# Attention scores from rounded parts: three one-pass products, with the two halves of the array's rows in turns

## The chip, the cores and the metric

The kernel runs on one core of a Trainium2 chip. Its time is the device time of one execution in microseconds (us). Beside the timed runs there is one execution taken by the hardware profiler: its page and its trace are what is read here. TensorE is the matrix engine (PE for its matmuls, PEld for its loads of stationary operands), VectorE is DVE, ScalarE is ACT, GpSimd is POOL, SyncE is SP.

## The reference, cut to what matters

The program is a block with a mixer, a cross attention and 32 experts, and then a second block of four layers, on 256 tokens of 1024 features in fp32. The four layers are a differential attention, a latent attention, a dilated attention and a differential attention again, each followed by a feed-forward network. The change is in the differential and the dilated ones.

```
def diff_attention(...):                       # 16 query and key heads of 64, 8 value heads of 128
    s = einsum('bhqd,bhkd->bhqk', q, k)        # contraction over 64
    p = softmax(s).reshape(B, 8, 2, S, S)
    a = p[:, :, 0] - lam * p[:, :, 1]
    o = einsum('bhqk,bhkd->bhqd', a, v)

def dilated_attention(...):                    # 3 groups of 16 heads of 64
    for window, dilation in ((128, 1), (512, 4), (2048, 16)):
        s = einsum(..., q, k)                  # banded, within a phase of the dilation
        lse = logsumexp(s);  p = exp(s - lse);  o = p v
    o = sum over groups of softmax(lse over groups) * o
```

## The kernel before, in words

All projections are fp32 products taken as three products of rounded parts. `split` (L186 to L199) makes of fp32 weights a high part on ScalarE (`whi`, L197) and the rest on VectorE (`wlo`, L198), both in the type float32r, which TensorE takes in one pass; `mm3` (L201 to L206) adds high by high, high by low and low by high. What is multiplied by weights is split likewise when it leaves PSUM, by `evac_split` (L208): a copy on ScalarE (L211), a subtraction on VectorE (L212). The scores, though, are products of plain fp32 tiles: TensorE takes such a product as two instructions.

The contraction of a score is over 64 features, so that a head fills half of the rows of the array, and two heads lie in one tile of 128 partitions: rows 0 to 63 and rows 64 to 127.

A differential layer (`attn_a`) has a written plan of steps: F is a piece of a projection (12 matmuls with 512 columns), S the scores of a pair of heads and their softmax (L1018 issues the products), T the transposes of the probabilities, V the values, O their transposes, W a piece of the output projection. Queries and keys are projected by token, turned by `rope` and transposed on TensorE into PSUM (`transposed_heads`, L961), from where ScalarE copies them into `qT` and `kT` (L962). For each half of the tokens the products go to the two halves of the rows by turns.

The dilated layer (`attn_c`) works in four rounds of four heads. `proj` makes queries, keys and values of the round; `heads` is called after it for the round before. In `heads`, for each of two pairs of heads, for each head s and each half of the tokens t (a score block), the products of the three groups go into one bank of PSUM (L1282: 256 columns for the first group, 128 for the others); VectorE adds the mask and takes the maximum (L1286), negates it (L937), ScalarE takes the exponential (L939), VectorE divides by the sum (L1291, L1292), TensorE transposes (L1295) into `tpp`, and ScalarE copies the result out (L1296). When four blocks are done the values follow (L1304, `po`). I call one call of `heads` a heads pass. The score banks share a pool of two with other products, and the probability rows `pr` one of two buffers.

The order on each engine is not that of the code: a scheduler lays the instructions out when the program is built, by its own idea of when each can start, and each engine then works through its list strictly in order. So a change of one product's form moves the instructions around it.

Of the kernel before, what the change touches and what calls it, by code (L numbers as in the profile page):

```python
# [9 lines left out]
F32 = mybir.dt.float32  # L10
F32R = mybir.dt.float32r
# [25 lines left out]
class Norm:  # L37
    """rows += scale * acc, by halves of the columns; rows * g transposed into hh, hl (or the halves hh); the rstd per token."""
# [48 lines left out]
class LastNorm(Norm):  # L87
    """rows += scale * acc; rms(rows) * g to the output."""
# [25 lines left out]
class Kernel:  # L114
# [39 lines left out]
    def load(self, *names, cuts=1, inner=RAW, ordered=False):  # L154
        """Start the loads of units of weights, as they lie in DRAM, by turns in so many cuts (of each `inner` columns)."""
# [18 lines left out]
    def raw(self, name):  # L174
        """The next unit of weights."""
        if self.ahead:
            n, t = self.ahead.pop(0)
            assert n == tuple(name), (n, name)
            return t
        return self.load(name)[0]  # L180
# [5 lines left out]
    def split(self, view, shape):  # L186
        """fp32 weights as the exact sum of two float32r parts."""
# [13 lines left out]
    def mm3(self, out, lh, ll, rh, rl, start, stop):  # L201
        """out += (lh + ll)^T (rh + rl), the product of the two low parts aside."""
# [14 lines left out]
    def gain(self, ap, n=D, pool=None, tag="gain"):  # L217
        """A gain vector on every partition."""
# [4 lines left out]
    def rstd(self, ss, n, eps, w=1):  # L223
        """(ss / n + eps) ** -0.5 for [P, w]."""
# [7 lines left out]
    def squares(self, x, out):  # L232
        """out [128, 1] = the sum of the squares of x [128, 512]."""
# [7 lines left out]
    def spread(self, r):  # L241
        """[128, 2] by token -> [128, 256]: token along the row, on every partition."""
# [16 lines left out]
    def phase1(self):  # L259
        nc, tc, A = self.nc, self.tc, self.A  # L260
        with ExitStack() as ctx:
            # what is done with first lies lowest: there the experts' weights land
# [3 lines left out]
            # memory: its rows in a buffer of weights, keys feature-major  # L266
# [16 lines left out]
            # x, wholly normalised  # L283
# [23 lines left out]
    def blocks(self, unit, acc, hh, hl, k0, nk, ncol, first, last):  # L307
        """acc[t][n] += h[:, k-tiles] @ unit, unit [P, nk, ncol], activations stationary:
        the pieces of it by bank, each to be called."""
# [24 lines left out]
    def finish(self, banks, acc, norm):  # L334
        """The last products of a sum, a bank after the other, into the norm that follows."""
# [14 lines left out]
    def proj_B(self, unit, hh, hl, evac):  # L350
        """unit [P, 8, 512] as stationary: evac(bank, f0) gets [128 features, 2, 256 tokens]."""
# [15 lines left out]
    def mixer(self, ctx, hh, hl):  # L367
# [7 lines left out]
        vec = m.tile([P, 5, 4], F32, name="mixvec")   # conv taps, g_conv_out, g_fft_out by feature  # L375
# [3 lines left out]
        # u, token-major  # L379
# [1138 lines left out]
```

## Time and profile before

| | |
|---|---|
| median of 3 timed runs | 2599.82 us (2599.73 to 2604.89) |
| span of the profiled execution, first to last instruction | 2597.9 us |
| what lies around the span (median less span) | 1.9 us |
| TensorE busy | 2518.0 us, 97% |
| VectorE, ScalarE busy | 1119.9 us (43%), 954.6 us (37%) |
| DMA, share of 16 engines on the large queue | 65.3% |
| mean granted clock of TensorE | 0.997 |

The profiled execution is one of its own; its own time is known as its span. The busy shares are means over stages that differ: the experts (from 220 to 1180 us) move weights at over 420 GB/s, the second block moves 110 to 200 GB/s and works on TensorE. In a timeline each row has its start, its duration, engine, line, operation and tiles, and the number of like instructions that were merged; matmuls overlap, so the pitch from start to start tells what one costs, and a row's duration includes the tail of its last one.

### The profile page before, as it was taken

How to read it: one execution, taken by the hardware profiler on the slowest of the kernel's cores; microseconds unless marked ns; L12 is line 12 of the kernel's file. 1: busy time of each engine (PE TensorE's matmuls, PEld its weight loads, DVE VectorE, ACT ScalarE, POOL GpSimd, SP SyncE). 2: the span in 40 equal slices, each digit the busy share in tenths (PEclk: the TensorE clock that was granted, in tenths of full speed). 3: DMA queues.
4: the chain of work that ended last, by engine and by line, in shares of the span. 5: the costliest groups of instructions: out<-in, count | busy, mean ns of one | idle time of the engine just before them, and what ended most of it. 6: DMA issues, size and time to landing. Idle time of an engine off the chain costs nothing.

```text
span 2597.9 us, 34064 instructions
## 1 busy us (share of the span) xinstructions
PE 2518.0 (97%) x14280; PEld 1769.4 (68%) x14280; DVE 1119.9 (43%) x1716; ACT 954.6 (37%) x1583; POOL 123.8 (5%) x256
## 2 busy tenths in 40 slices
PE   8999999999999999999999999999999999999998
PEld 7885333333333333337799978998888899977997
DVE  5643211111111111126655656555555565566555
ACT  5451000000000001016644575445555544466443
POOL 0000000000000000002100020001111100021000
PEclk9999999999999999999999999999999999999999
DMA  9458999999999999994344433555334355543453
GB/s 359 143 190 322 379 427 417 424 428 428 427 428 427 427 428 427 370 421 173 115 180 176 182 129 134 195 195 195 127 134 146 134 199 183 199 164 113 174 192 114
DMA packets 55277, 677.03 MB, mean 261 GB/s; under 512 B 8112, under 2 KB 10800, under 8 KB 14416
## 3 DMA queue, kind: packets, MB, share of 16 engines
q1 hardware_dynamic: 54976, 674.29, 65.3%
q8 instruction: 114, 1.87, 0.3%
q10 hardware_dynamic: 144, 0.52, 0.1%
q14 instruction: 43, 0.35, 0.0%
HBM read 673.74 MB, written 1.05 MB: 260 GB/s over the span
## 4 chain that ended last, share of the span: by engine, by line
PE 47%; issue 8%; DVE 2%; ACT 1%; POOL 1%; DMA 1%; POOLq 0%; SPq 0%; ACTq 0%
PE pj L204 5%; PE pj L206 5%; PE pj L205 5%; PE pb L206 4%; PE pb L205 4%; PE pb L204 4%; PE acc L204 3%; PE acc L205 3%; PE acc L206 3%; PE sc L1282 1%; PE pg L672 1%; PE pu L672 1%; PE py L750 1%; DVE wlo L198 1%; PE po L1304 1%
## 5 line engine op out<-in xcount | busy, mean ns | idle before, releaser
L198 DVE TENSOR_TENSOR wlo<-raw,whi 128x1024 fp32r<-128x1024 f32 (+1 forms) x491 | 603.1, 1230 | 473.6 <-ACT whi L197 473.0
L197 ACT ACTIVATE whi<-raw 128x1024 fp32r<-128x1024 f32 (+1 forms) x491 | 515.1, 1050 | 602.1 <-PE pb L205 250.7
L204 PE MATMUL pb<-hhi,whi 128*128 128x256 f32 x1504 | 427.0, 284 | 0.5 <-ACT whi L197 0.4
L205 PE MATMUL pb<-hlo,whi 128*128 128x256 f32 x1504 | 426.5, 284 | 0.6 <-DVE hlo L212 0.6
L206 PE MATMUL pb<-hhi,wlo 128*128 128x256 f32 x1504 | 426.3, 283 | 0.0
L204 PEld LDWEIGHTS pb<-hhi,whi 128*128 128x128 f32 x1504 | 289.1, 192 | 3.2 <-ACT whi L197 0.8
L205 PEld LDWEIGHTS pb<-hlo,whi 128*128 128x128 f32 x1504 | 289.2, 192 | 2.6 <-DVE hlo L212 1.0
L206 PEld LDWEIGHTS pb<-hhi,wlo 128*128 128x128 f32 x1504 | 289.2, 192 | 0.6 <-DVE wlo L198 0.6
L672 PE MATMUL pg<-raw,xt 128*64 128x512 f32 x1024 | 240.4, 595 | 0.0
L750 PE MATMUL py<-raw,at 128*64 128x512 f32 x1024 | 240.3, 593 | 0.0
L672 PE MATMUL pu<-raw,xt 128*64 128x512 f32 x1024 | 232.2, 592 | 0.0
L204 PE MATMUL pj<-whi,hhi 128*128 128x512 f32 (+3 forms) x544 | 208.8, 384 | 0.4 <-ACT hhi L211 0.4
L206 PE MATMUL pj<-whi,hlo 128*128 128x512 f32 (+3 forms) x544 | 204.5, 376 | 0.0
L205 PE MATMUL pj<-wlo,hhi 128*128 128x512 f32 (+3 forms) x544 | 203.9, 375 | 0.0
L750 PEld LDWEIGHTS py<-raw,at 128*64 128x64 f32 x1024 | 85.2, 137 | 140.1 <-issue 140.1
L672 PEld LDWEIGHTS pu<-raw,xt 128*64 128x64 f32 x1024 | 76.7, 137 | 145.0 <-issue 144.9
L672 PEld LDWEIGHTS pg<-raw,xt 128*64 128x64 f32 x1024 | 76.1, 137 | 145.5 <-issue 144.8
L761 DVE TENSOR_TENSOR x<-pc,x 128x512 f32<-128x512 f32 x64 | 44.2, 692 | 257.6 <-PE pc L759 257.6
L204 PE MATMUL acc<-whi,ah 128*128 128x512 f32 x352 | 137.7, 391 | 0.0
L205 PE MATMUL acc<-wlo,ah 128*128 128x512 f32 x352 | 137.5, 391 | 0.0
L206 PE MATMUL acc<-whi,al 128*128 128x512 f32 x352 | 137.1, 389 | 0.0
L229 POOL TENSOR_TENSOR rr<-rv,mhalf 128x2 f32<-128x2 f32 (+1 forms) x36 | 26.3, 730 | 2203.9 <-DVE rv L227 2186.2
(297 smaller groups left out, 3164.2 us busy)
## 6 DMA issues: line engine op xcount, KB each, us to landing
raw<-in_w_moe SPq DMA_DIRECT2D x190, 2048.0 KB, 16.6
raw<-in_f_gu SPq DMA_DIRECT2D x44, 2048.0 KB, 8.4
raw<-in_f_out SPq DMA_DIRECT2D x24, 2048.0 KB, 8.2
raw<-in_a_qkv SPq DMA_DIRECT2D x12, 2048.0 KB, 8.3
raw<-in_c_qk SPq DMA_DIRECT2D x12, 2048.0 KB, 8.4
raw<-in_w_in SPq DMA_DIRECT2D x4, 2048.0 KB, 15.6
raw<-in_a_wo SPq DMA_DIRECT2D x4, 2048.0 KB, 7.9
raw<-in_c_v SPq DMA_DIRECT2D x4, 2048.0 KB, 8.4
```

Of the source, the lines that this page charges most:

```text
L197: nc.scalar.activation(h3, view, AF.Copy)
L198: nc.vector.tensor_tensor(l3, view, f32(h3), op=OP.subtract)
L204: mm(out, lh, rh, start=start, stop=False)
L205: mm(out, lh, rl, start=False, stop=False)
L206: mm(out, ll, rh, start=False, stop=stop)
L229: nc.gpsimd.tensor_tensor(r, v, self.mhalf[:, :w], op=OP.pow)
L672: nc.tensor.matmul(ps[j * 64:(j + 1) * 64, :], xt[:, kk, c0:c0 + CAP], w[:, k, j * 512:(j + 1) * 512], start=late and kk == 0, stop=not la ...
L750: nc.tensor.matmul(py[n][i * 64:(i + 1) * 64, :], at[i][:, k, u * 64:(u + 1) * 64], w[i][:, k, n * 512:(n + 1) * 512], start=u == 0 and k ...
L761: nc.vector.tensor_tensor(xs, ps, xs, op=OP.add)
L1282: nc.tensor.matmul(o, qT[sl, g * 2 + hp, ts], kT[sl, g * 2 + hp, :] if g == 0 else kT[sl, g * 2 + hp, ts], start=True, stop=True)
L1304: nc.tensor.matmul(po[s * 64:(s + 1) * 64, t * P:(t + 1) * P], v[:, kt, g, h * 64:(h + 1) * 64], pTs[s][:, t, b, :], start=b == 0, stop=b ...
```

## The change

Transposed queries and keys are kept as a high and a low part in float32r instead of one fp32 tile. A new helper, `scores`, makes each score as three one-pass products, and gives each of the three to both heads of a pair before the next. For this the dilated layer fills two banks together, one for each head, where it filled them one after the other. The comments and docstrings go as well, which moves line numbers and nothing else.

```diff
     def transposed_heads(self, src, ident, w, n, dst, t):
...
-            nc.scalar.activation(dst[:w, b0:b0 + nb, t * P:(t + 1) * P],
-                                 tp[:w, :nb * P].rearrange("p (a b) -> p a b", a=nb), AF.Copy)
+            v = tp[:w, :nb * P].rearrange("p (a b) -> p a b", a=nb)
+            if isinstance(dst, tuple):
+                self.evac_split(v, *(d[:w, b0:b0 + nb, t * P:(t + 1) * P] for d in dst))
+            else:
+                nc.scalar.activation(dst[:w, b0:b0 + nb, t * P:(t + 1) * P], v, AF.Copy)
+
+    def scores(self, ps, q, k):
+
+        for a, b in ((0, 0), (0, 1), (1, 0)):
+            for s in range(2):
+                sl = slice(s * 64, (s + 1) * 64)
+                self.nc.tensor.matmul(ps[s], q[a][sl], k[b][sl], start=a + b == 0, stop=a == 1)
...
     def attn_a(self, ctx, i, h, nxt):
...
-            qT, kT = (w2.tile([P, 4, S], F32, tag=f"T{c}", name=self.nm("qkT")) for c in range(2))
+            qT, kT = (tuple(w2.tile([P, 4, S], F32R, tag=f"T{c}{d}", name=self.nm("qkT")) for d in range(2)) for c in range(2))
...
             for t in range(2):
-                for s in range(2):
-                    sl = slice(s * 64, (s + 1) * 64)
-                    nc.tensor.matmul(ps[s][:, t * S:(t + 1) * S], qT[sl, p, t * P:(t + 1) * P], kT[sl, p, :],
-                                     start=True, stop=True)
+                self.scores([x[:, t * S:(t + 1) * S] for x in ps], [x[:, p, t * P:(t + 1) * P] for x in qT], [x[:, p, :] for x in kT])
...
     def attn_c(self, ctx, i, h, nxt):
...
-            qT = w2.tile([P, 6, S], F32, tag="qT", name=self.nm("qT"))
-            kT = w2.tile([P, 6, S], F32, tag="kT", name=self.nm("kT"))
+            qk = [tuple(w2.tile([P, 4, S], F32R, tag=f"qk{d}", bufs=4, name=self.nm("qk")) for d in range(2)) for _ in range(3)]
...
-                        nc.scalar.activation(qT[:, g * 2:g * 2 + 2, t * P:(t + 1) * P], t4[:, 0:2, :], AF.Copy)
-                        nc.scalar.activation(kT[:, g * 2:g * 2 + 2, t * P:(t + 1) * P], t4[:, 2:4, :], AF.Copy)
+                        self.evac_split(t4, *(x[:, :, t * P:(t + 1) * P] for x in qk[g]))
...
             for hp in range(2):
-                pTs = []
-                for s in range(2):
-                    pT = w2.tile([P, 2, 4, P], F32, tag="pT", name=self.nm("pT"))
-                    for t in range(2):
-                        ts = slice(t * P, (t + 1) * P)
-                        sl = slice(s * 64, (s + 1) * 64)
-                        ps = self.bank(self.nm("sc"))
-                        for g in range(3):
-                            o = ps[:, 0:256] if g == 0 else ps[:, 128 + g * P:256 + g * P]
-                            nc.tensor.matmul(o, qT[sl, g * 2 + hp, ts], kT[sl, g * 2 + hp, :] if g == 0 else kT[sl, g * 2 + hp, ts],
-                                             start=True, stop=True)
+                pTs = [w2.tile([P, 2, 4, P], F32, tag="pT", name=self.nm("pT")) for _ in range(2)]
+                for t in range(2):
+                    ts = slice(t * P, (t + 1) * P)
+                    pss = [self.bank(self.nm("sc")) for _ in range(2)]
+                    for g in range(3):
+                        o = slice(0, 256) if g == 0 else slice(128 + g * P, 256 + g * P)
+                        self.scores([x[:, o] for x in pss], [x[:, hp, ts] for x in qk[g]],
+                                    [x[:, 2 + hp, :] if g == 0 else x[:, 2 + hp, ts] for x in qk[g]])
+                    for ps, pT in zip(pss, pTs):
```

TensorE at the start of the first heads pass of the dilated layer, before. `sc` is a bank of scores, `pj` a bank of a projection, `tpp` one of transposed probabilities; sc_12248, sc_12268 and sc_12289 are three score blocks of one head or the other.

```order
L1282 MATMUL sc_12248<-kT_11819,qT_11818 128x256
L1282 MATMUL sc_12248<-kT_11819,qT_11818 128x128 x2
L1282 MATMUL sc_12268<-kT_11819,qT_11818 128x256
L1282 MATMUL sc_12268<-kT_11819,qT_11818 128x128 x2
L1282 MATMUL sc_12289<-kT_11819,qT_11818 128x256
L1282 MATMUL sc_12289<-kT_11819,qT_11818 128x128 x2
L204 MATMUL pj_12454<-whi_12456,hhi_11682 128x512
L205 MATMUL pj_12454<-wlo_12457,hhi_11682 128x512
L206 MATMUL pj_12454<-whi_12456,hlo_11683 128x512
```

Each row here is one product, of two instructions each on the chip.

The same place in the changed kernel, from the last two instructions of the first two blocks on (sc_12329 for rows 0 to 63, sc_12330 for rows 64 to 127); sc_12381 and sc_12382 are the next two blocks, in the same two banks.

```order
L973 MATMUL sc_12329<-qk_11898,qk_11899 128x128
L973 MATMUL sc_12330<-qk_11898,qk_11899 128x128
L204 MATMUL pj_12586<-whi_12588,hhi_11758 128x512
L205 MATMUL pj_12586<-wlo_12589,hhi_11758 128x512
L206 MATMUL pj_12586<-whi_12588,hlo_11759 128x512
L973 MATMUL sc_12381<-qk_11894 128x256
L973 MATMUL sc_12381<-qk_11895,qk_11894 128x256
L973 MATMUL sc_12381<-qk_11894,qk_11895 128x256
L973 MATMUL sc_12381<-qk_11896 128x128
L973 MATMUL sc_12381<-qk_11897,qk_11896 128x128
L973 MATMUL sc_12382<-qk_11894 128x256
L973 MATMUL sc_12382<-qk_11895,qk_11894 128x256
```

The first two blocks go by turns, eighteen instructions in all; after three projection matmuls the next two begin, five of one half and then five of the other. A little later in the changed kernel:

```order
L973 MATMUL sc_12382<-qk_11897,qk_11896 128x128
L973 MATMUL sc_12381<-qk_11896,qk_11897 128x128
L973 MATMUL sc_12382<-qk_11896,qk_11897 128x128
L973 MATMUL sc_12381<-qk_11898 128x128
L1298 MATMUL tpp_12359<-ident,pr_12349 128x128 x4
L973 MATMUL sc_12382<-qk_11898 128x128
L1298 MATMUL tpp_12375<-ident,pr_12365 128x128 x4
L973 MATMUL sc_12381<-qk_11899,qk_11898 128x128
```

The transposes of the first two blocks' probabilities (pr_12349, pr_12365) now stand within the next two blocks' scores, with no projection work beside them. In a whole heads pass the scores lie in ten separate stretches, and in seven before.

VectorE at the same place, before. ISA is the masked maximum of a score block (L1286), `wlo` the low part of projection weights, `nb` the negated maximum, `rs` the reciprocal of the sum.

```order
L1286 ISA pr_12252,mx_12253<-sc_12248,mask 128x512
L1286 ISA mx_12253 128x1
L198 TENSOR_TENSOR wlo_12505<-raw_12452,whi_12504 128x1024
L937 TENSOR_SCALAR nb_12256<-mx_12253 128x1
L1286 ISA pr_12272,mx_12273<-sc_12268,mask 128x512
L1286 ISA mx_12273 128x1
L937 TENSOR_SCALAR nb_12276<-mx_12273 128x1
L1291 RECIPROCAL rs_12259<-sm_12255 128x1
L1292 TENSOR_SCALAR pr_12252<-pr_12252,rs_12259 128x512
```

And VectorE in the changed kernel:

```order
L198 TENSOR_TENSOR wlo_12637<-raw_12584,whi_12636 128x1024
L1289 ISA pr_12349,mx_12350<-sc_12329,mask 128x512
L1289 ISA mx_12350 128x1
L1289 ISA pr_12365,mx_12366<-sc_12330,mask 128x512
L1289 ISA mx_12366 128x1
L937 TENSOR_SCALAR nb_12353<-mx_12350 128x1
L937 TENSOR_SCALAR nb_12369<-mx_12366 128x1
L1294 RECIPROCAL rs_12356<-sm_12352 128x1
L1295 TENSOR_SCALAR pr_12349<-pr_12349,rs_12356 128x512
```

The split of the weights stands ahead of the first maximum, and both blocks' maxima stand ahead of both negations.

In the differential layers, TensorE at the second pair of heads of the first layer, in the changed kernel (sc_6059 and sc_6060 are its two heads, qkT the four tiles of queries and keys); before, these four products stand together, by turns but for two pairs in each layer.

```order
L973 MATMUL sc_6059<-qkT_5754,qkT_5752 128x256
L973 MATMUL sc_6059<-qkT_5755,qkT_5752 128x256
L973 MATMUL sc_6059<-qkT_5754,qkT_5753 128x256
L973 MATMUL sc_6059<-qkT_5754,qkT_5752 128x256
L973 MATMUL sc_6059<-qkT_5755,qkT_5752 128x256
L973 MATMUL sc_6059<-qkT_5754,qkT_5753 128x256
L206 MATMUL pj_6101<-whi_6104,hlo_5649 128x512
L973 MATMUL sc_6060<-qkT_5754,qkT_5752 128x256
```

All six of one half come first here, and a projection matmul lies between the halves. Other pairs keep the turns, and three of eight are cut in two after the first two instructions.

## Rows read from the trace of the kernel before

**Rows 1.** The page's busy time, share of the span and instructions of TensorE

```profile
PE 2518.0 (97%) x14280; PEld 1769.4 (68%) x14280; DVE 1119.9 (43%) x1716; ACT 954.6 (37%) x1583; POOL 123.8 (5%) x256
```

**Rows 2.** Busy time by stretch: length, engines with instructions, clock, DMA share, GB/s

```profile
1185.00:1285.00 100.00, 93.31 (x486) 72.68 (x486) 63.68 (x157) 64.31 (x158) 21.29 (x40) 1.00 0.38 141
1830.00:2075.00 245.00, 244.95 (x1470) 203.03 (x1469) 126.81 (x228) 138.95 (x237) 35.20 (x72) 1.00 0.36 132
...
1836.03:1859.16 23.13, 23.12 (x170) 18.14 (x169) 15.44 (x44) 14.40 (x30) 0.00 (x0) 1.00 0.25 91
```

**Rows 3.** Timeline of TensorE at the first scores of layer 0: start, duration, instruction

```profile
1199.50 0.40 PE L206 MATMUL pj<-whi,hlo 128*128 128x512 f32 x1
1199.83 1.13 PE L1018 MATMUL sc<-qkT,qkT 64*128 64x256 f32 x8
1200.89 0.50 PE L204 MATMUL pj<-whi,hhi 128*128 128x512 f32 x1
1201.23 0.40 PE L205 MATMUL pj<-wlo,hhi 128*128 128x512 f32 x1
1201.47 0.40 PE L206 MATMUL pj<-whi,hlo 128*128 128x512 f32 x1
```

**Rows 4.** The same timeline, cut to one moment within the eight

```profile
1200.37 0.38 PE L1018 MATMUL sc<-qkT,qkT 64*128 64x256 f32 x2
```

**Rows 5.** Timeline of TensorE at the start of the first heads pass

```profile
1835.70 0.28 PE L205 MATMUL pj<-wlo,hhi 128*128 128x256 f32 x1
1835.82 0.28 PE L206 MATMUL pj<-whi,hlo 128*128 128x256 f32 x1
1836.03 3.07 PE L1282 MATMUL sc<-kT,qT 64*128 64x256 f32 x18
```

**Rows 6.** Timeline of VectorE there

```profile
1837.21 0.69 DVE L1286 CUSTOM_DVE_ANT_0 pr<-sc,mask 128x512 f32<-128x512 f32 x1 [1.63 <-PE sc L1282]
...
1837.82 1.22 DVE L198 TENSOR_TENSOR wlo<-raw,whi 128x1024 fp32r<-128x1024 f32 x1
```

**Rows 7.** Timeline of ScalarE there

```profile
1836.51 1.05 ACT L197 ACTIVATE whi<-raw 128x1024 fp32r<-128x1024 f32 x1
```

**Rows 8.** Timeline of VectorE ten microseconds on, two blocks behind each other

```profile
1846.26 0.69 DVE L1286 CUSTOM_DVE_ANT_0 pr<-sc,mask 128x512 f32<-128x512 f32 x1 [0.34 <-PE tpp L1295]
1846.87 0.08 DVE L1286 DVE_READ_ACCUMULATOR2_ANT mx<- 128x1 f32 x1
1846.93 0.69 DVE L1286 CUSTOM_DVE_ANT_0 pr<-sc,mask 128x512 f32<-128x512 f32 x1
...
1847.55 0.27 DVE L937 TENSOR_SCALAR nb<-mx 128x1 f32<-128x1 f32 x2
...
1848.84 0.49 DVE L1292 TENSOR_SCALAR pr<-pr,rs 128x512 f32<-128x512 f32 x1
```

**Rows 9.** Timeline of TensorE there: the values and the transposes that follow

```profile
1846.91 1.97 PE L1304 MATMUL po<-pT,v 128*64 128x128 f32 x32
...
1849.47 0.63 PE L1295 MATMUL tpp<-ident,pr 128*128 128x128 f32 x4
```

**Rows 10.** Groups by line and shape: busy us, mean ns of one, idle before

```profile
L212 DVE TENSOR_TENSOR hlo<-tp,hhi 128x512 fp32r<-128x512 f32 x44 | 28.5, 683 | 0.6 <-ACT hhi L211 0.5
...
L1261 ACT ACTIVATE kT<-tpq 128x256 f32<-128x256 f32 x24 | 9.3, 386 | 0.0
```

**Rows 11.** Waits before the dilated layer's score products (L1282): us in total, times

```profile
  DVE rs L1291: 2.1, 8
```

**Rows 12.** Timeline of TensorE at transposes of queries and keys of layer 0

```profile
1231.63 0.63 PE L961 MATMUL tpq<-ident,q 128*128 128x128 f32 x4 [1.80 <-DVE ssa L1056]
1233.52 0.63 PE L961 MATMUL tpq<-ident,q 128*128 128x128 f32 x4 [1.26 <-DVE o L1060]
```

**Rows 13.** Busy time by stretch, at the same transposes of the last layer

```profile
2336.00:2340.40 4.40, 1.31 (x8) 0.71 (x7) 3.52 (x11) 2.63 (x8) 0.70 (x1) 1.00 0.94 400
2340.50:2343.80 3.30, 3.30 (x13) 2.81 (x12) 0.76 (x1) 0.97 (x2) 0.00 (x0) 0.50 0.04 10
```

More of the change, by code (lines that the diff above doesn't have):

```diff
@@ L1268, in proj, with heads @@
                                          scale=r[:, t:t + 1])
-            return qT, kT, v
-        def heads(qd, qT, kT, v):
+            return qk, v
+        def heads(qd, qk, v):
             for hp in range(2):
-                pTs = []
-                for s in range(2):
-                    pT = w2.tile([P, 2, 4, P], F32, tag="pT", name=self.nm("pT"))
-                    for t in range(2):
-                        ts = slice(t * P, (t + 1) * P)
-                        sl = slice(s * 64, (s + 1) * 64)
-                        ps = self.bank(self.nm("sc"))
-                        for g in range(3):
-                            o = ps[:, 0:256] if g == 0 else ps[:, 128 + g * P:256 + g * P]
-                            nc.tensor.matmul(o, qT[sl, g * 2 + hp, ts], kT[sl, g * 2 + hp, :] if g == 0 else kT[sl, g * 2 + hp, ts],
-                                             start=True, stop=True)
+                pTs = [w2.tile([P, 2, 4, P], F32, tag="pT", name=self.nm("pT")) for _ in range(2)]
[7 more added lines that the diff above has]
+                    for ps, pT in zip(pss, pTs):
                         pr = w2.tile([P, 1, 512], F32, tag="pr", name=self.nm("pr"))
@@ L1296, in heads @@
                         nc.scalar.activation(pT[:, t], tp.rearrange("p (b q) -> p b q", b=4), AF.Copy)
-                    pTs.append(pT)
                 po = self.bank(self.nm("po"))
```

## The prediction

> **What bounds the kernel now.** I read the page's busy line first: TensorE is busy for 97% of the span [rows 1]. A busy TensorE is not always TensorE at its peak, so next I read the busy time by stretch. The dilated layer (1830 to 2075) has TensorE at 244.95 of 245.00 us, and the first differential layer (1185 to 1285) at 93.31 of 100.00 [rows 2]. VectorE and ScalarE are at half to two thirds in both. So the end is set by how long TensorE's in-order queue takes: by the pitch of its matmuls (start to start), by what it loses when it changes between whole-array and half-array work, and by the few places where it waits. Last came the timelines around the scores.
>
> In the differential layers the eight score instructions of a pair of heads (four products, two passes each) take 1.13 us and the last of them 0.38 [rows 3, 4]. Two of them share one 0.38 us stretch [rows 4]: the two halves of the rows already run side by side there, since the loop over the halves is the inner one. A pair of instructions comes every 0.22 us. Around them, the step from the projection to the scores is 0.33 instead of the projection's usual 0.23, the first pair takes 0.10 more than the others, the step back is 0.31 instead of 0.22, and the next projection's is 0.34 instead of 0.23 [rows 3]: about 0.41 us for each excursion into the half-array form.
>
> In the dilated layer the halves follow each other. Eighteen score instructions, that is three of the eight blocks of one heads pass, take 3.07 us [rows 5], or about 0.90 a block without the tail of the last one and the first load. A heads pass (four heads by two halves of the tokens are eight score blocks, with their softmax rows, transposes and values) lasts 23.13 us [rows 2], and there are four.
>
> **The change part by part.** *Transposed queries and keys, now two tiles.* ScalarE's copy out of PSUM stays (16 in the differential layers, and 24 whole ones in place of 48 halves of 0.39 us); VectorE gains 40 subtractions of 128x512 at 0.68 us [rows 10], 27 us in all. In the dilated layer they lie beside projections that last tens of microseconds before the first score reads them, so I take nothing. In the differential layers the first pair of heads waits for them; the order there puts six projection matmuls between the first pair of score passes and the rest, and that is the cover; without it a subtraction of 0.68 us would stand open once in each half of each layer.
>
> *The score products in the dilated layer.* Each is now three one-pass instructions instead of two two-pass ones: 72 for a heads pass instead of 48. A rounded product of 256 columns has a pitch of 0.12 us [rows 5]. No row has a rounded one of 128 columns. From below, it can't be under about 0.06 (half of 0.12); from above, it costs what the unrounded product of 128 columns does, (0.90 - 2 x 0.22) / 4 = 0.115 for each of two instructions, 0.23. I take 0.12, because the unrounded 128-column instruction, with the same weights to load, has 0.115. In the order, the first block pair alternates by instruction (nine pairs), but of the other three block pairs each begins with four or five passes of one half, then as many of the other. Counting a pair of both halves as one step and a lone one as one, a pass has 9 + 14 + 14 + 13 = 50 steps: 6.0 us, against 8 x 0.90 = 7.2. That is -1.2 us a pass.
>
> *Changes of form.* The order has ten stretches of half-array work in a pass where it had seven, at 0.41 us each [rows 3]: +1.2.
>
> *The wait that takes the place.* This term decides. Both banks of the scores are now filled together, and the next block pair needs both again. VectorE has to read bank A, then bank B. In the order the split of the last weights (wlo) now stands ahead of the first of these reads; before, it stood behind it. It can start when ScalarE's split ends, at 1836.51 + 1.05 = 1837.56 [rows 7], that is 1.5 us after the first score, and takes 1.22 [rows 6], so the read of A runs from 2.75 to 3.4 us instead of from 1.2 [rows 5, 6]. TensorE meanwhile has 0.1 + 9 x 0.12 = 1.2 of scores, a step back and three projection matmuls, and wants bank A at 2.1 us. Wait: 1.4 us.
>
> Next, the transposes of the probabilities. From the read of A's scores to the transpose in the trace, with both reads one behind the other: the read of A starts at 1846.26, the read of B at 1846.93, both negated maxima follow at 1847.55, then the exponential, and the scaling at 1848.84; the transpose starts at 1849.47 [rows 8, 9]. From the end of A's read, where its maximum is taken over at 1846.87, that is 2.6 us. Before, in that place, TensorE had 32 value matmuls of 1.97 us [rows 9] to do in it. Now the next block pair starts at the end of A's read and gives TensorE 13 score passes, 11 to 12 steps or 1.45 us with the first load, and a change of 0.2, 1.65 in all: it waits about 1.0 us. That comes three times a pass, at the three block pairs after the first. The remaining waits for a bank come to about 0.1 and 0.4 at the third and fourth pair, and 0.2 each at the switch to bank B (the second read ends 0.6 us after the first, the five passes of A last 0.6 to 0.7): 0.9 together. Sum 1.4 + 3 x 1.0 + 0.9 = 5.3 us; from this go the waits of now, 2.1 us in 8 places over four passes [rows 11], 0.5 a pass. So +4.8. Behind each of these waits stands TensorE's whole queue, so that nothing fills them; ScalarE and VectorE have the next weights' splits behind them, which wait for TensorE in turn.
>
> The Trainium skill speaks against the change in the same way: its page "TensorEngine Tiling (Array Packing)", section "PSUM Bottleneck", says that tiling quickens TensorE but not the emptying of PSUM, which can become the bound. By that rule nothing of a quicker score is kept; it has no price, so the sum goes by the rows above.
>
> *Sum of a pass:* -1.2 + 1.2 + 4.8 = +4.8 us; four passes, +19.2 us.
>
> *The score products in the differential layers.* Per layer, eight pairs of heads. Before: six of eight alternate, 0.41 + 4 x 0.22 = 1.29 us; two go by halves, 0.41 + 7 x 0.22 = 1.95: 11.6 us. After: thirteen excursions (five pairs are cut in two, two of them with all of one half before the other) and 6 x 6 + 2 x 12 = 60 steps of 0.12: 5.3 + 7.2 = 12.5. So +0.9. Against it, two projection matmuls (0.46 us) now stand between two groups of transposes, where TensorE sat idle for 1.26 us [rows 12]. That leaves +0.45 a layer, +0.9 for the two; I keep -2 and +4 as ends, since the waits between these pieces can fall either way.
>
> Span 2597.9 + 19.2 + 0.9 = 2618.0. The timed runs' median of 2599.82 lies 1.9 above the profiled span, which lies outside of the first and last instruction and stays: 2620 us.
>
> **The rivals.** *A, the softmax rows keep up* (the other side). If the splits of the weights leave VectorE's queue earlier than I think, and the chain of 2.6 us shrinks to the 1.65 that TensorE can fill, the 4.8 us of waiting goes: -1.2 + 1.2 a pass, and with 128-column passes at 0.06 another -1.5 for the 29 steps of that width, -6 us: 2594; without that, 2600. It decides when A's bank is read within 2.1 us of the first score. For it: the present waits are only 0.5 us a pass. Against it: the split stands ahead in the order, and the rows of the chain are of instructions whose work isn't changed. The Trainium skill's "TensorEngine Tiling (Array Packing)", section "Theoretical Speedup", gives up to twice the speed for contractions of at most 64 rows. Taken alone it would halve the 7.2 us of scores, -14 us in four passes, 2586; of A's chance I give it 0.02, since the rows show a VectorE that reads one bank in 0.6 us and can't be asked for two sooner.
>
> *B, rounded passes of 128 columns cost as much as the unrounded product*, 0.23. 29 steps by 0.11 add 3.2 us a pass, of which the 1.0 us waits behind 13 passes take up some 0.6 three times and the others a little: +1.1 a pass, 2624 to 2625.
>
> *C, rounded passes of the two halves don't run side by side.* The 12 or so steps that are pairs in the first block pair and at the ends of the others become two: about +2.5 us a pass, half of it inside waits, and 3 us in the differential layers: 2627; with B, 2633.
>
> *D, the clock.* After two gaps in 2336 to 2340.4, with TensorE busy for 1.31 of 4.40 us, the granted clock was 0.50, the lower of its two levels, for the next 3.3 [rows 13]. The waits above leave TensorE busy for over half of the time. If it falls all the same, each fall doubles the steps of some 3 us: up to 1.7 us, and 7 for one in each pass: 2626.
>
> **Chances.** Forecast 0.55, B 0.20, C 0.08, D 0.05 (all slower), A 0.12, split in no change 0.07 and faster 0.05. Within 0.2% (5.2 us) is about what a measurement of this kernel can't tell from no change. So slower 0.88, same 0.07, faster 0.05. The range: from below, the first wait of 1.4 us missing in all passes and the differential layers at -2 give 2611, and a little of A is let in, 2610; from above B with C, 2633.
>
> **What would show it.** In the changed profile: in the dilated layer, waits of TensorE's weight loads for the score bank on the masked maximum, and for the transposes on the scaling of the probabilities, together 21 us against 2.1 for the scores now; a heads pass of 28 us instead of 23; the layer longer by 19 and the two differential ones within 2 us of now; the feed-forward stretches unchanged. The step of 128-column passes can be read in the first nine pairs: 18 instructions in 1.4 us with the tail if 0.12 holds, in 1.9 or more by B or C. I am wrong if the waits after the scores stay near 0.5 us a pass, or if the transposes start within 5.3 us of the pass's first score, as they do now.

## The result, and the profile after

The changed kernel takes 2630.94 us (median of 4 runs, 2627.93 to 2634.10) against 2599.95 of the kernel before on the same chip: 1.0117 times as long, 95% interval 1.0105 to 1.0129. It is slower, as forecast, by 31 us where I had 20. Two of its four executions (2632.87, the profiled one, and 2634.10) and one of the four before (2604.89) are some 5 us longer than the others of their kernel, and like against like the difference is 28.6 us.

The profiled execution has a span of 2631.1 us, 33.2 more than before. By stretches of the trace the feed-forward network and the dilated layer behind it have 28.0 of these. Layer 0 has 2.8 more and layer 3 with the feed-forward ahead of it 1.9 less (the profile of before had a clock fall there, [rows 13]); the experts and what lies ahead of them, whose code isn't changed, have 4.3 more, with a clock fall of 6.8 us among the experts that the profile of before lacks. The page's busy line answers to [rows 1]; TensorE is busy for 23 us longer, with 160 matmuls more:

```profile
PE 2541.2 (97%) x14440; PEld 1785.5 (68%) x14440; DVE 1141.6 (43%) x1756; ACT 954.0 (36%) x1559; POOL 121.6 (5%) x256
```

The stretch from the feed-forward of the latent layer to the end of the dilated one, and layer 0, before (stretch, length, then busy time and instructions of PE, PEld, DVE, ACT, POOL, then granted clock, DMA share, GB/s):

```profile
1606.70:2098.90 492.20, 492.15 (x3084) 429.55 (x3083) 270.99 (x382) 259.36 (x391) 49.22 (x98) 1.00 0.45 162
...
1186.80:1304.60 117.80, 112.48 (x623) 91.09 (x624) 78.06 (x179) 75.64 (x178) 20.26 (x37) 1.00 0.39 142
```

The same two after, then the first heads pass (it answers to the last of [rows 2]), and four stretches, one in each heads pass:

```profile
1613.80:2134.00 520.20, 508.69 (x3181) 441.46 (x3180) 283.45 (x406) 258.89 (x367) 49.20 (x98) 0.95 0.42 153
1191.10:1311.70 120.60, 115.79 (x656) 94.20 (x657) 83.72 (x190) 75.74 (x178) 18.27 (x37) 0.97 0.38 139
1843.09:1874.40 31.31, 28.46 (x197) 22.17 (x196) 14.94 (x44) 14.72 (x30) 0.00 (x0) 0.78 0.19 68
1848.00:1861.70 13.70, 12.97 (x75) 10.03 (x74) 4.10 (x14) 4.78 (x12) 0.00 (x0) 0.50 0.33 135
1926.50:1936.70 10.20, 10.20 (x54) 7.66 (x53) 3.13 (x11) 3.91 (x8) 0.00 (x0) 0.50 0.35 143
2001.60:2015.30 13.70, 12.99 (x74) 9.98 (x74) 4.10 (x14) 4.78 (x12) 0.00 (x0) 0.50 0.33 135
2080.10:2090.30 10.20, 10.20 (x54) 7.66 (x54) 3.19 (x11) 3.91 (x8) 0.00 (x0) 0.50 0.35 143
```

In each pass the granted clock is 0.50 for 10 or 14 us, 47.8 us in all, where the layer had none before. TensorE is busy for 46.4 us of them. I estimate that this work takes half as long at the upper level (the values below take 3.68 us in place of 1.97), so the slow clock costs 23.2 us. The idle time is 520.20 - 508.69 = 11.5 us. The rest, 508.69 - 23.2 = 485.5, is 6.6 less than before. So 28.0 = 11.5 waiting + 23.2 slow clock - 6.6 less work, the last two by that estimate. The first pass lasts 31.3 us where I had 28.

The waits of TensorE there are the forecast ones, and only these (us in total, times, longest); they answer to [rows 11]:

```profile
PE tpp L1298 <- DVE pr L1295: 6.1, 8, 0.8
PE sc L973 <- DVE mx L1289: 5.3, 4, 1.3
```

TensorE's timeline at the start of the first pass answers to [rows 5, 9]:

```profile
1843.09 0.39 PE L973 MATMUL sc<-qk 64*128 64x256 f32 x2
1843.31 0.40 PE L973 MATMUL sc<-qk,qk 64*128 64x256 f32 x4
1843.55 0.22 PE L973 MATMUL sc<-qk 64*128 64x128 f32 x2
1843.61 0.39 PE L973 MATMUL sc<-qk,qk 64*128 64x128 f32 x4
1843.83 0.28 PE L973 MATMUL sc<-qk 64*128 64x128 f32 x2
1843.94 0.39 PE L973 MATMUL sc<-qk,qk 64*128 64x128 f32 x4
1844.26 0.51 PE L204 MATMUL pj<-whi,hhi 128*128 128x512 f32 x1
...
1846.55 0.38 PE L973 MATMUL sc<-qk 64*128 64x256 f32 x1 [1.33 <-DVE mx L1289]
...
1848.80 1.11 PE L1298 MATMUL tpp<-ident,pr 128*128 128x128 f32 x4 [0.73 <-DVE pr L1295]
...
1857.83 3.68 PE L1306 MATMUL po<-pT,v 128*64 128x128 f32 x32
```

The eighteen products take 1.17 us to the next projection. Then 1.33 us without work for the bank, 0.73 more for the softmax, and between the two the clock falls: the same values that took 1.97 us [rows 9] take 3.68. Just ahead of the fall TensorE was busy for 1.47 of 2.80 us:

```profile
1845.10:1847.90 2.80, 1.47 (x14) 1.35 (x13) 2.20 (x7) 0.69 (x2) 0.00 (x0) 1.00 0.54 94
```

VectorE's timeline there answers to [rows 6, 8]:

```profile
1844.66 1.23 DVE L198 TENSOR_TENSOR wlo<-raw,whi 128x1024 fp32r<-128x1024 f32 x1 [2.02 <-ACT whi L197]
1845.80 0.68 DVE L1289 CUSTOM_DVE_ANT_0 pr<-sc,mask 128x512 f32<-128x512 f32 x1
...
1846.41 0.69 DVE L1289 CUSTOM_DVE_ANT_0 pr<-sc,mask 128x512 f32<-128x512 f32 x1
...
1848.26 0.49 DVE L1295 TENSOR_SCALAR pr<-pr,rs 128x512 f32<-128x512 f32 x1
```

The split of the weights runs first, and the maximum of the first bank 2.7 us after the pass began, as forecast.

### The profile page after: what moved, and what is told of

It reads as the page before. It is cut to its first block, busy times and chain, and to the rows that moved or that the text cites. A ratio compares the mean times of both kernels' runs of the same rounds, so it can differ in the third digit from the quotient of the medians.

```text
span 2631.1 us, 34392 instructions
## 1 busy us (share of the span) xinstructions
PE 2541.2 (97%) x14440; PEld 1785.5 (68%) x14440; DVE 1141.6 (43%) x1756; ACT 954.0 (36%) x1559; POOL 121.6 (5%) x256
## 4 chain that ended last, share of the span: by engine, by line
PE 46%; issue 8%; DVE 3%; ACT 2%; POOL 1%; DMA 0%; POOLq 0%; SPq 0%; ACTq 0%
PE pj L204 5%; PE pj L206 5%; PE pj L205 5%; PE pb L206 4%; PE pb L205 4%; PE pb L204 4%; PE acc L206 3%; PE acc L204 3%; PE acc L205 3%; PE pg L672 1%; PE pu L672 1%; PE py L750 1%; PE sc L973 1%; PE tpp L1298 1%; DVE wlo L198 1%
## 5 line engine op out<-in xcount | busy, mean ns | idle before, releaser
L680 ACT ACTIVATE sg<-gs 128x512 f32<-128x512 f32 x32 | 20.1, 630 | 303.9 <-DVE gs L678 303.9
```

Source lines behind the costliest of these rows:

```text
L680: nc.scalar.activation(sg, gs, AF.Sigmoid, scale=1.702)
```

## The experiments

The theory: the scheduler leaves too little projection work between the rounded scores and what waits for their softmax; TensorE waits, the clock falls, and both cost. Rivals: the bank pairs, the rounded products themselves, the differential layers.

**Differential layers alone** (the dilated layer as before).

```diff
     def attn_c(self, ctx, i, h, nxt):
-            qk = [tuple(w2.tile([P, 4, S], F32R, tag=f"qk{d}", bufs=4, name=self.nm("qk")) for d in range(2)) for _ in range(3)]
+            qT = w2.tile([P, 6, S], F32, tag="qT", name=self.nm("qT"))
+            kT = w2.tile([P, 6, S], F32, tag="kT", name=self.nm("kT"))
...
```

> The differential layers as in the changed kernel, the dilated layer as before. Theory 1 (the loss sits in the dilated layer: TensorE waits for the softmax rows there, and its clock falls behind these waits): within 3 us of before, 2597 to 2603, a few us more only where a clock fall lies in layer 0 (the changed kernel's profile has two of 3.4 us there). Rival (the cut-up score groups of the differential layers carry a part of the 31 us): 2605 to 2612, layer 0 at 120 us or more without a clock fall.

Measured: 2600.23 us (11 runs) against 2600.04, ratio 0.9998 (0.9989 to 1.0007). The differential layers cost nothing that can be measured. Its profiled execution (2604.33) has the changed kernel's clock falls among the experts (6.8 us) and in layer 0 (two of 3.4 us), with a dilated layer as long as before. So these falls don't belong to the loss in that layer.

**Rounded products, one bank after the other.**

```diff
...
-                for t in range(2):
...
-                    pss = [self.bank(self.nm("sc")) for _ in range(2)]
+                for s in range(2):
...
+                    for t in range(2):
...
+                        ps = self.bank(self.nm("sc"))
...
+                            for a, b in ((0, 0), (0, 1), (1, 0)):
+                                nc.tensor.matmul(ps[:, o], q[a], k[b], start=a + b == 0, stop=a == 1)
```

> The changed kernel, but in the dilated layer the three rounded products are made block after block, one bank at a time, as the loop of before had it. Theory 1 (too little projection work stands between the scores and the transposes that wait for their softmax, since the scores as the scheduler counts them fill that place): the order still has only three projection matmuls there, so the time stays at 2620 to 2635, with waits on the scaling of the probabilities and a granted clock of 0.5 in each heads pass. Rival (two banks filled together are the cause): back within 6 us of before, 2597 to 2606, clock 1.0 in the dilated layer.

Measured: 2647.98 us, ratio 1.0181 (1.0164 to 1.0198): 17 us above the changed kernel, more than either theory had. Its waits in the layer, then the two half-clock stretches of its first pass and the whole stretch of feed-forward and dilated layer:

```profile
PE sc L1290 <- DVE mx L1293: 4.8, 4, 1.2
PE tpp L1302 <- DVE pr L1299: 4.6, 8, 0.6
PE tpp L1302 <- DVE nb L937: 2.3, 4, 0.6
```

```profile
1843.70:1857.40 13.70, 13.03 (x73) 10.77 (x73) 5.00 (x18) 5.01 (x13) 0.00 (x0) 0.50 0.31 132
1860.70:1867.50 6.80, 6.42 (x19) 5.00 (x20) 2.48 (x8) 2.65 (x6) 0.00 (x0) 0.50 0.00 0
...
1609.40:2149.40 540.00, 527.97 (x3181) 463.07 (x3180) 285.83 (x406) 259.83 (x367) 49.27 (x98) 0.92 0.41 148
```

The waits come to 11.7 us, about as after, but each pass has 20.5 us at half clock where the changed kernel has 10 to 14: 34 us more in four passes. If TensorE is busy in all four as in the first (19.45 us), that is 31 us more of busy half speed, and by the same estimate 16 of the 19.8 us by which the stretch is longer than after (540.0 against 520.2). So filling the banks in pairs isn't the loss. What pairing by itself gives back isn't shown: the scheduler's order changed with it, and no projection matmul is left ahead of the first wait, where the changed kernel has three.

**Pairs of banks, plain fp32 products** (the differential layers as in the changed kernel).

```diff
...
-                        self.scores([x[:, o] for x in pss], [x[:, hp, ts] for x in qk[g]],
-                                    [x[:, 2 + hp, :] if g == 0 else x[:, 2 + hp, ts] for x in qk[g]])
+                        for s in range(2):
+                            sl = slice(s * 64, (s + 1) * 64)
+                            nc.tensor.matmul(pss[s][:, o], qk[g][sl, hp, ts], qk[g][sl, 2 + hp, :] if g == 0 else qk[g][sl, 2 + hp, ts],
+                                             start=True, stop=True)
```

> The changed kernel, but in the dilated layer the two banks are filled together with plain fp32 products of two instructions, heads in turns. The order then has eight projection matmuls behind the first pair of blocks and one or two ahead of the transposes. Theory 1: 2595 to 2603, no clock fall in the dilated layer, waits under 1 us a pass. Rival (banks in pairs): 2615 to 2630, waits for the bank on the masked maximum as in the changed kernel. Rival (the rounded products themselves are dear): as theory 1; the woven kernel tells these two apart.

Measured: 2593.97 us (10 runs), ratio 0.9979 (0.9969 to 0.9989), a little below what theory 1 had. The whole stretch, without a clock fall, and TensorE's timeline at its first pass:

```profile
1613.60:2099.70 486.10, 484.81 (x3084) 422.02 (x3083) 270.24 (x382) 258.28 (x367) 49.22 (x98) 1.00 0.45 164
...
1842.98 1.15 PE L1286 MATMUL sc<-qk 64*128 64x256 f32 x12
1844.05 0.50 PE L204 MATMUL pj<-whi,hhi 128*128 128x512 f32 x1
...
1845.78 0.39 PE L205 MATMUL pj<-wlo,hhi 128*128 128x512 f32 x1
1846.43 1.75 PE L1286 MATMUL sc<-qk 64*128 64x256 f32 x12 [0.26 <-DVE mx L1291]
```

Two blocks in plain fp32 take 1.07 us to the next projection, where the rounded ones take 1.17. Behind them stand eight projection matmuls, where the changed kernel has three, and the wait for the bank is 0.26 instead of 1.33. So rounding a paired score gains nothing here.

**The same rounded products in a written order.**

```diff
+    plan_c = "F S0 F F S1 F T0 F S2 F T1 V0 F S3 F T2 F F T3 F V1"
...
+            for step in plan.split():
+                if step == "F":
+                    fs.pop(0)()
+                else:
+                    steps[step]()
```

F is a piece of the next round's projection, S a pair of score blocks, T its transposes, V the values. The last round, which has no next, has pieces of the output projection. The probabilities have four buffers instead of two, and the output projection is cut into pieces for this, so that more than the order changes.

> The changed kernel's rounded score products in pairs, but the dilated layer by a written plan: 12 to 24 projection matmuls (2.6 us and more) of the next round stand between each pair of score blocks and the next, and between the scores and their transposes. Theory 1: the waits on the masked maximum and on the scaling are covered, the clock stays at 1.0, and the dilated layer falls from about 272 us to 245 or less: 2588 to 2600 in all. Rival (the three-pass products cost the time themselves): the scores still take the time and the total stays above 2612. Rival (the clock falls by the mix of half-array work and not by the waits): stretches at 0.5 remain in each pass, 2605 to 2620.

Measured: 2589.23 us, ratio 0.9951 (0.9936 to 0.9967), 42 us under the changed kernel with the same score products. The stretch of feed-forward and dilated layer, its waits, and two of the waits in TensorE's timeline:

```profile
1609.00:2091.30 482.30, 475.25 (x3181) 418.55 (x3181) 281.06 (x406) 254.55 (x367) 48.73 (x98) 1.00 0.45 165
```

```profile
PE tpp L1314 <- DVE qk L212: 5.2, 3, 1.8
PE tpp L1314 <- ACT pT L1315: 1.8, 1, 1.8
```

```profile
1864.66 0.66 PE L1314 MATMUL tpp<-ident,pr 128*128 128x128 f32 x4 [1.76 <-DVE qk L212]
...
2050.79 0.38 PE L973 MATMUL sc<-qk,qk 64*128 64x128 f32 x4
2052.96 1.14 PE L1314 MATMUL tpp<-ident,pr 128*128 128x128 f32 x8 [1.78 <-ACT pT L1315]
```

No wait is put down to a masked maximum or a scaling any more, the clock is 1.00, and there are as many matmuls as after (3181). So the form of the products isn't the loss. The stretch is 37.9 us shorter than after: 4.5 less waiting (7.1 against 11.5), the 23.2 of slow clock, and 475.25 instead of 485.5 us of work, 10 less. The next kernel changes the order alone. Four waits of 1.7 to 1.8 us are left, and none is followed by a clock fall, not even the last, which stands right behind a pair of score blocks. So the length of a wait alone doesn't bring the clock down.

**The same plan without cover** (three of the four passes).

```diff
-    plan_c = "F S0 F F S1 F T0 F S2 F T1 V0 F S3 F T2 F F T3 F V1"
+    plan_c = "F F F F S0 S1 T0 S2 T1 V0 S3 T2 T3 V1"
```

> The woven kernel with one line of its plan changed: in three of the four heads passes all steps of scores, transposes and values follow each other without a piece of projection between them, as the changed kernel has them by its scheduler; the pieces come ahead of the pass and behind it. The same work, another order. Theory 1 (order: waits on the softmax rows, and the clock that falls behind them): waits of 2 to 5 us and a stretch of 10 us or more at a clock of 0.5 in each of the three passes, 15 to 24 us above the woven kernel: 2604 to 2613. Rival (the rounded products, or the layout of the changed kernel, cost by themselves): the order changes nothing, 2587 to 2593.

Measured: 2605.77 us (10 runs), ratio 1.0021 (1.0012 to 1.0031): 16.5 us above the woven kernel for one line of the plan. TensorE's timeline in its first pass, then a piece of that pass and the whole stretch:

```profile
1848.92 0.39 PE L206 MATMUL pj<-whi,hlo 128*128 128x512 f32 x1
1851.16 0.44 PE L973 MATMUL sc<-qk 64*128 64x256 f32 x1 [1.85 <-DVE mx L1300]
...
1853.88 1.97 PE L1314 MATMUL tpp<-ident,pr 128*128 128x128 f32 x8
1855.77 0.59 PE L973 MATMUL sc<-qk 64*128 64x256 f32 x2
```

```profile
1851.30:1861.50 10.20, 10.12 (x62) 8.96 (x64) 6.17 (x25) 6.20 (x15) 0.18 (x1) 0.50 0.30 103
...
1606.90:2105.70 498.80, 490.88 (x3181) 433.50 (x3180) 283.00 (x406) 257.21 (x367) 49.21 (x98) 0.97 0.44 160
```

After one wait of 1.85 us the clock is 0.50 for 10.2 us, and within these the transposes follow their scores without a wait: at half speed TensorE takes 2.7 us over the pair of blocks (1851.16 to 1853.88), longer than the 2.4 us that the chain of the softmax took after. The slow clock hides the waits that I had forecast there. Idle time is 7.9 us, 0.9 more than in the woven kernel; three such stretches of 10.2 us at half speed are, by the estimate of half, 15 of the 16.5. Without these 15 its work is 475.7 us, as in the woven kernel. So the cover is worth 16.5 of the 42 us, as waits and slow clock; the 10 us less work of the woven kernel come from what the two have in common.

**Useless work in the gaps.** The tight kernel with matmuls whose result is used nowhere, six, four and three behind the first three pairs of scores.

```diff
+                for n in range({"S0": 6, "S1": 4, "S2": 3}.get(step, 0) if qd < 3 else 0):
+                    idle = self.bank(self.nm("pj")) if n == 0 else idle
+                    nc.tensor.matmul(idle, hh[:, 0, 0:P], hh[:, 0:2, :].rearrange("p a b -> p (a b)"), start=True, stop=True)
```

> The tight kernel with 13 matmuls of 512 columns in each of the three passes whose result is used nowhere, six behind the first pair of scores, four behind the second, three behind the third: where TensorE would wait. That is 39 x 0.23 = 9 us more of TensorE's work. If the stretches at half clock cost time of their own, they go (clock 1.0 in the layer) and the kernel is no slower than the tight one, or faster: -5 to +2 us against it. If they cost nothing, because TensorE only walks slowly through time in which it would else have waited for the softmax rows, the useless work shows by what the waits don't cover: +3 to +9 us. If the clock falls all the same, it isn't the waits that bring it down: +9 or more.

Measured: 2602.85 us (10 runs), ratio 1.0011 (1.0002 to 1.0020): 2.9 us less than the tight kernel with 9 us more to do. The two intervals overlap, but eight of the ten runs lie below every run of the tight kernel, and the stretches in the profiles say the same, 495.8 against 498.8:

```profile
1606.50:2102.30 495.80, 489.53 (x3219) 428.71 (x3218) 282.43 (x406) 257.07 (x367) 49.07 (x98) 1.00 0.44 161
```

```profile
PE sc L973 <- DVE mx L1300: 4.2, 6, 1.2
```

The clock is 1.00: with work in the gaps it no longer falls, and the falls cost time of their own. Not every gap is gone: a wait of 1.2 us for the bank is left in each of the three passes, now behind six whole-array matmuls, and the clock doesn't fall behind it.

**Six useless matmuls instead of thirteen** (four and two).

> The tight kernel with six useless matmuls of 512 columns in each of the three passes in place of thirteen: four behind the first pair of scores, two behind the second. 18 x 0.23 = 4 us more of TensorE's work, nearly all within waits. If it is the waits' length that brings the clock down and the falls that cost, the clock stays at 1.0 and it is 3 to 6 us quicker than the kernel with thirteen (2602.85): 2597 to 2600. If the clock falls all the same, the second and later waits count too, and it comes out where the tight kernel does or above, 2604 to 2610.

Measured: 2602.64 us (11 runs), ratio 1.0010 (1.0001 to 1.0019), between the two expectations. Its profiled execution still has 6.8 us at half clock in two of the three passes, with waits of up to 1.6 us for the bank: what it saves in work it may lose to the clock. It separates nothing further.

**One gap only.** The woven plan with the second pair of scores right behind the first.

```diff
-    plan_c = "F S0 F F S1 F T0 F S2 F T1 V0 F S3 F T2 F F T3 F V1"
+    plan_c = "F S0 S1 F F F T0 F S2 F T1 V0 F S3 F T2 F F T3 F V1"
```

> The woven kernel with the second pair of scores put right behind the first in three of the four heads passes (the two pieces of projection between them come behind the second pair), and all other steps covered as there. It leaves one wait in a pass, for the bank on the masked maximum, as it was 1.85 us in the tight kernel. If a single wait of this length ahead of a stretch of dense work is enough to bring the clock to 0.5 for some 10 us, each pass has such a stretch, and the price is the wait and half of what is done at half clock: 3 x (1.85 + 5) = 21 us above the woven kernel's 2589, 2605 to 2612. If it takes a wait and thin work behind it (half-array products and transposes), or several waits, the clock stays at 1.0 and only the wait is paid: 3 x 1.85 = 5.5 us, 2593 to 2597; a short fall of 3.4 us in each pass would be between, 2598 to 2602.

Measured: 2600.06 us (10 runs), ratio 1.0002 (0.9992 to 1.0011), 10.8 us above the woven kernel; it fits the case between, in time, though two of the falls are twice as long as I gave that case. TensorE's timeline in the second pass, and the whole stretch with its three falls:

```profile
1911.70 0.38 PE L973 MATMUL sc<-qk 64*128 64x256 f32 x1 [0.97 <-DVE mx L1300]
...
1914.80 0.63 PE L205 MATMUL pj<-wlo,hhi 128*128 128x512 f32 x1
1915.23 0.63 PE L206 MATMUL pj<-whi,hlo 128*128 128x512 f32 x1
```

```profile
1606.70:2099.30 492.60, 485.15 (x3180) 426.41 (x3179) 280.38 (x406) 255.83 (x367) 49.24 (x98) 0.98 0.45 162
1844.30:1847.70 3.40, 3.40 (x9) 2.65 (x9) 2.58 (x10) 1.70 (x5) 0.00 (x0) 0.50 0.36 149
1912.60:1919.40 6.80, 6.80 (x25) 5.62 (x25) 4.01 (x14) 3.68 (x9) 0.00 (x0) 0.50 0.40 169
1984.30:1991.10 6.80, 6.80 (x24) 5.52 (x23) 4.20 (x15) 3.63 (x9) 0.00 (x0) 0.50 0.37 152
```

Here one wait of 0.97 us in each of three passes is followed by a fall each time. Half-array scores stand on both sides of it, with three projection matmuls ahead of it and dense projections soon after. The 1.2 us in the kernel with useless work, and the 1.7 to 1.8 us in the woven one, were not followed by a fall. So what stands around a wait counts too; what of it decides, the runs don't show. The idle time is 7.5 us against 7.1 in the woven kernel, since other waits of that kernel became shorter; the 17.0 us at half clock, all of them busy, cost, by the estimate of half, 8.5 of the 10.3 by which the stretch is longer.

**Woven with plain products, and then without any rounded score.** The third edit above, in the woven plan; then the differential layers as before too.

> The woven plan with plain fp32 score products of two instructions in the dilated layer, in pairs of the two halves. Tells what rounding the scores is worth once the order is good. By the pitches of the traces a pair of score blocks is 4 x 0.22 for plain products and about 0.85 for nine rounded pairs, so nothing of it is gained by rounding, and the plain form is spared 24 subtractions of 0.68 us on VectorE and the waits of the last round behind them: 2586 to 2590, the same as the woven kernel's 2589 or up to 3 us less. Rival (rounded products are what makes the woven kernel quick): 2592 to 2597.

> The woven plan with plain products as just above, and the differential layers as before too, so that no rounded score is left. If the cut-up score groups of the differential layers cost the 1 to 3 us that their segments show (119 to 121 us against 118 for layer 0, with one or two clock falls of 3.4 us), this is the fastest of all: 2584 to 2588. Rival (layer 3 gives back what layer 0 loses): the same as the kernel just above within 1.5 us.

Measured: 2585.94 us, ratio 0.9947 (0.9933 to 0.9960), and 2585.03, ratio 0.9945 (0.9931 to 0.9958), both at the lower end of what was expected or just below. They are 0.9 us apart with intervals that overlap, so they don't tell whether the cut-up score groups of the differential layers cost anything. The second beats both kernels, by 15 us the one before and by 46 the changed one. Its stretch:

```profile
1605.50:2083.90 478.40, 474.51 (x3084) 414.55 (x3083) 266.33 (x382) 254.02 (x367) 48.74 (x98) 1.00 0.45 167
```

It has 0.7 us less of TensorE's work than the woven kernel's 475.25, and 3 us less of idle time: rounding the scores buys nothing here.

## Why the prediction was right, and where it was off

*Direction and place.* Right: the loss lies in the dilated layer, and it begins with the wait named, for bank A behind the split of the weights. I had 1.4 us for it; it is 1.33 in each of the four passes. That the time lies inside the range is in part luck: the upper end of 2633 was made of rivals B and C, which are both out, and the sum came near because the slow clock, which isn't in it, took the place of waits that didn't come.

*The transposes' waits, 3 x 1.0, and the other bank waits, 0.9 a pass.* Too high by more than half: two of 0.7 to 0.8 us a pass, and none of the others. All the waits are 11.4 us where I had 21. The chain of the softmax was right, 1848.80 - 1846.41 = 2.4 us against 2.6; but behind the first of these waits TensorE runs at half speed, and the chain catches up with it.

*The clock, rival D.* This is the step that failed: I gave it 0.05, and a price from falls of 3.3 us [rows 13], on the ground that the waits would leave TensorE busy for over half of the time. They did (1.47 of 2.80 us ahead of the first fall), and it fell all the same, in every pass, for 10.2 or 13.7 us. So the 19.2 us of the forecast, nearly all of them waits, are in truth 11.5 of waits and 23.2 of work at half speed, less 6.6. Rival D's sum for one fall in each pass was 2626, between forecast and result. The Trainium skill has the mechanism, in "TensorE: Matmul & The Clock Gate", section "A second HAM failure mode: psum-queue depth-cycling": short idle times between groups of matmuls that take turns at PSUM banks make the clock go up and down. The trace of the changed kernel agrees, with 1.33 us of wait for a bank and 13.7 us at 0.50; the useless work's kernel has waits of 1.2 us for the same bank and no fall, so which such waits do it stays open.

How much the waits would be at full clock stays open. The tight kernel shows only that its falls cost at least 3 us net, and that they stand where waits would have stood.

*Scores and changes of form, 0 in sum.* By the estimate of half, the work apart from waits and clock came out 6.6 us smaller in four passes. The paired plain kernel, at full clock, has 484.81 us where before had 492.15: a saving of this size comes without any rounded score in the layer.

*Rivals B and C.* Both are out: the nine pairs take 1.17 us to the next projection, with pitches of 0.06 to 0.12 behind the first pair. (In the text of C "the 12 or so steps" is a slip: by the prediction's own counts 72 - 50 = 22 steps are pairs, and 22 x 0.12 gives its 2.5 us.) *Rival A*, that the softmax keeps up, is out for this order; in the woven one no wait is put down to a softmax row. The rule that I had set beside the forecast, "PSUM Bottleneck" in the Trainium skill's "TensorEngine Tiling (Array Packing)", doesn't bind where enough other work stands in between: the paired plain kernel takes 1.07 us for two blocks where before took 1.8, and is 6 us quicker.

*The differential layers, +0.9.* Within what can be measured: the medians are 0.2 us apart, and the interval of the ratio goes from -2.9 to +1.8 us.

## What to carry to other kernels

A product that gets quicker, or that the scheduler counts differently, moves the work that stood behind it: look at what now fills the time until its reader is done, and write the order out where the chain is longer than the fill. Price a wait of TensorE with the clock that may fall behind it: in one kernel here one wait of 0.97 us made a heads pass 3.6 us longer (10.8 by 3), while longer waits in the woven one brought no fall. When a stretch shows a low clock and no waits, don't conclude that nothing waits: slow work may just hide it.

## What the runs showed of the hardware that I had not expected

- Gaps of 0.97 to 1.85 us, with half-array work around them, were followed by a granted clock of 0.50 (1.2 GHz in place of 2.4) for 3.4 to 13.7 us. Waits of 1.7 to 1.8 us in the woven kernel, one right behind half-array scores, were not. With useless matmuls in the gaps it stayed at 1.00, and the kernel was 2.9 us quicker for 9 us more work.
- Rounded pairs of 128 columns follow each other at 0.11 us, hardly quicker than those of 256 columns at 0.12; the one right behind the first 128-column pair starts after 0.06 (1843.55 to 1843.61). So it isn't the columns alone that set 0.11; what does, the runs don't show.
